# A decoder layer's opening: row products taken before the norm, the norm put in at their eviction, loads in another order, TensorE given transposes at the start

## The chip, the cores and the metric

The kernel runs on one core of one Trainium2 chip. The metric is device time in microseconds (us), taken over the whole program; fewer is better. Five engines work side by side, each through its own list of instructions in a fixed order: TensorE (PE: matmuls and transposes), VectorE (DVE), ScalarE (ACT), GpSimd (POOL) and SyncE (SP, which here issues the loads). They wait for each other by semaphores. PE writes into PSUM, which this kernel uses as eight banks of 128 x 512 floats: three with the tag `mm`, four with `at`, one with `o`. Everything else lives in SBUF.

## The reference, cut to what matters

A hybrid decoder layer on 512 rows of width 1024. What the change touches is the opening: the normed input `h`, its projections, and the keys and values of the memory.

```python
h = rms_norm(x, g_mix)                       # x * rsqrt(mean(x*x)) * g_mix, row by row
proj = h @ w_in                              # (512 x 1024) @ (1024 x PROJ_WIDTH)
q, k, v, qi, ki, wi, conv_in, qc, gate_pre = split_cols(proj, PROJ_SIZES)
qi, ki = partial_rope(qi), partial_rope(ki)  # index heads; score = sum_h wi * relu(qi . ki), top-256 keys
bg, cg, u = split(conv_in, 3)
y_conv = (bg * causal_dwconv(cg * u, conv_w_short)) @ w_conv_out
mem_kv = rms_norm(mem, g_mem) @ w_mem_kv     # keys and values of the 256 memory tokens
```

After that come attention, gates, an output projection, and a gated MLP with a causal convolution; the change leaves them as they are.

## The kernel before, in words

Every product is done in three matmuls. Both factors are split into a high part (the value rounded to the format fp32r) and a low part (what is left over), and `mm3` (L150 to L152) adds high x high, high x low and low x high. A split costs two instructions: ACT writes the high part (`whi`, `hhi`), DVE subtracts it from the source to give the low part (`wlo`, `hlo`). A projection `project(c0)` is 24 matmuls of 512 columns: eight slices k of the 1024 rows, three matmuls each, into one `mm` bank. The next weight tile is loaded by SP into one of three `raw` buffers and split by ACT and DVE.

The opening runs in this order. `x_n` holds, per slice k, the transposed x (512 columns), the 424 weight columns that need rows on the partitions (`wn`: v, the index queries and keys, and wi), and g_mix. `m_kv` holds the transposed memory, its 512 weight columns and g_mem.

1. The products of the memory (L295 to L299): 48 matmuls into two banks, `pkv[0]` (the `o` bank) and `pkv[1]` (an `mm` bank), as four loads of m_kv land.
2. The row norms: ACT squares the four tiles of x rows (L265), POOL takes the power (L269), DVE and ACT build a diagonal `dg`, high and low (L312, L315), and two matmuls with ones (L318) spread the norms over all partitions as `rb`, in PSUM.
3. For each slice k: DVE forms h = x * g_mix * rb (L345), ACT its high part (L348), DVE its low part (L351); every second k also splits `wn` (L347, L350). PE then does twelve matmuls of 424 columns (L354 to L358) into the four `at` banks. They are the row products, 96 in all. In between, ACT squares the two tiles of memory rows and evicts `kr` and `VM` from the two `pkv` banks.
4. The projections of the short convolution, three passes c over C_CG, C_U and C_BG. For c = 0 the three weight tiles are loaded ahead (`ahead`, L320 to L330). C_CG is evicted by ACT as `rr` (L520), C_U multiplied with it by DVE (L523), C_BG multiplied in later. PE's ten transposes of `rn` (the index queries and keys after rope, L390 and L392) come two matmuls after the start of C_U.
5. ACT lays the index queries and keys out for four-way packed products (`Q4`, `K4`, L444 and L455, with DMAs from SP for the low parts), and PE does the score matmuls (L463) in between the next projections.

What sets the order: the instructions in `keep(...)` stay in the order in which they are written; the others are placed by a scheduler that goes by its own model of when things are ready. On each engine the result is a fixed list. `bank("mm")` gives out three buffers; a product into a bank waits until what was in it has been read.

Of the kernel before, what the change touches and what calls it, by code (L numbers as in the profile page):

```python
# [93 lines left out]
def layer(ctx, tc, x, mem, g_ffn, g_final, w_in, x_n, m_kv, w_cm, w_att, w_o, w_up, w_down,  # L94
# [150 lines left out]
    mkv, rows = [], []
    for c in range(KD // 2):
        n = 1 if c == 0 else 2
        raw = op.tile([P, 2, M + 2 * CW + 1], F32, tag=kv_tags[c], name="mkv")
# [3 lines left out]
        if c == 2:
            rows += [first_rows(x, b, wp, "raw", 3) for b in range(2)]
    rows += [first_rows(x, 2, wp, "raw", 3), first_rows(x, 3, op, "omeh")]
    xn = []
    for c in range(KD // 2):
        raw = ea.tile([P, 2, S + NW + 1], F32, name=f"xn{c}")
        keep(nc.sync.dma_start(raw, x_n[2 * c:2 * c + 2].rearrange("k p c -> p k c")))
        xn.append(raw)
# [56 lines left out]
    rb = bank()  # L316
    for i in range(2):
        keep(nc.tensor.matmul(rb, ones_r, dg[:, i].rearrange("p b s -> p (b s)"), start=i == 0, stop=i == 1))  # L318

    ready = {}  # L320

    def ahead(c0):

        src = w_in[IN_STARTS.index(c0)]
        raw = wp.tile(list(src.shape), F32, tag="raw", name="raw", bufs=3)
        keep(nc.sync.dma_start(raw, src))
        hi = wp.tile(list(src.shape), F32R, tag="whi", name="whi", bufs=3)
        lo = wp.tile(list(src.shape), F32R, tag="wlo", name="wlo", bufs=3)
        keep(nc.scalar.activation(hi, raw, AF.Copy))
        keep(nc.vector.tensor_sub(lo, raw, hi.bitcast(F32)))  # L330
        ready[c0] = hi, lo


    kr = op.tile([P, MB, CW], F32, tag="oath", name="kr")
    rm = ea.tile([P, MB], F32, name="rm")
    vms = [pkv[b][:, CW:].rearrange("p (h d) -> p h d", d=HD) for b in range(MB)]
    pn = [bank("at") for b in range(NB)]
    for c, raw in enumerate(xn):
        wh = ea.tile([P, 2, NW], F32R, name=f"wnh{c}")
        wl = ea.tile([P, 2, NW], F32R, name=f"wnl{c}")  # L340
        w = raw[:, :, S:S + NW]
        for j in range(2):
            k = 2 * c + j
            xt = raw[:, j, :S]
            keep(nc.vector.scalar_tensor_tensor(xt, xt, raw[:, j, S + NW:], rb, op0=ALU.mult, op1=ALU.mult))  # L345
            if j == 0:
                keep(nc.scalar.activation(wh, w, AF.Copy))  # L347
            keep(nc.scalar.activation(h[0][:, k], xt, AF.Copy))  # L348
            if j == 0:
                keep(nc.vector.tensor_sub(wl, w, wh.bitcast(F32)))  # L350
            keep(nc.vector.tensor_sub(h[1][:, k], xt, h[0][:, k].bitcast(F32)))  # L351
            bs = [slice(b * P, (b + 1) * P) for b in range(NB)]
            for b in range(NB):
                keep(nc.tensor.matmul(pn[b][:, :NW], h[0][:, k, bs[b]], wh[:, j], start=k == 0, stop=False))  # L354
            for b in range(NB):
                keep(nc.tensor.matmul(pn[b][:, :NW], h[0][:, k, bs[b]], wl[:, j], start=False, stop=False))  # L356
            for b in range(NB):
                keep(nc.tensor.matmul(pn[b][:, :NW], h[1][:, k, bs[b]], wh[:, j], start=False, stop=k == KD - 1))  # L358

            if k in (4, 5):  # L360
                squares(memn[k - 4], ss[:, 1, k - 4:k - 3])
            if k == 5:
                power(ss[:, 1, :MB], rm)
            if k == 6:
                for b in range(MB):
                    keep(nc.scalar.activation(kr[:, b], pkv[b][:, :CW], AF.Copy, scale=rm[:, b:b + 1]))
                    keep(nc.scalar.activation(VM[:, b, :, 0:HD], vms[b], AF.Copy, scale=rm[:, b:b + 1]))
# [1 line left out]
    for b in range(MB):
        keep(nc.vector.scalar_tensor_tensor(VM[:, b, :, HD:], vms[b], rm[:, b:b + 1], VM[:, b, :, 0:HD].bitcast(F32),  # L370
                                            op0=ALU.mult, op1=ALU.subtract))
    rn = op.tile([P, NB, NIH + 1, IDXD], F32, tag="ocvl", name="rn")
# [540 lines left out]
```

## Time and profile before

| | us |
|---|---|
| time, median of 3 runs (lowest, highest) | 758.69 (757.86, 758.94) |
| the profiled execution's own time | 758.13 |
| its span in the trace | 756.3 |
| PE busy | 739.1 (98%) |
| DVE busy | 466.8 (62%) |
| ACT busy | 341.2 (45%) |

The profiled execution is one of its own; its 758.13 lies between the lowest and the highest of the three runs, 0.56 us below their median. The span goes from the first to the last instruction of the trace. In the slices of the page PE is at 9 tenths or more from the third of 40 slices to the last but one; only the first 38 us and the last slice have room. All that the change moves lies in the first 75 us.

### The profile page before, as it was taken

How to read it: one execution, taken by the hardware profiler on the slowest of the kernel's cores; microseconds unless marked ns; L12 is line 12 of the kernel's file. 1: busy time of each engine (PE TensorE's matmuls, PEld its weight loads, DVE VectorE, ACT ScalarE, POOL GpSimd, SP SyncE). 2: the span in 40 equal slices, each digit the busy share in tenths (PEclk: the TensorE clock that was granted, in tenths of full speed). 3: DMA queues.
4: the chain of work that ended last, by engine and by line, in shares of the span. 5: the costliest groups of instructions: out<-in, count | busy, mean ns of one | idle time of the engine just before them, and what ended most of it. 6: DMA issues, size and time to landing. Idle time of an engine off the chain costs nothing.

```text
span 756.3 us, 9061 instructions
## 1 busy us (share of the span) xinstructions
PE 739.1 (98%) x3428; PEld 616.7 (82%) x3428; DVE 466.8 (62%) x787; ACT 341.2 (45%) x566; POOL 17.4 (2%) x42
## 2 busy tenths in 40 slices
PE   6899999999999999999999999999999999999995
PEld 4788888888888888888899888888888888888884
DVE  4756999999777763385466565656565654121215
ACT  6658465686455543244235434343434343121214
POOL 0100002000000000000010000000000000000001
PEclk9999999999999999999999999999999999999998
DMA  9725234522122224244403232322223232323202
GB/s 340 285 95 181 84 113 125 168 66 81 56 92 74 73 74 177 92 140 140 139 29 102 94 100 96 94 101 90 105 87 109 86 110 81 114 84 111 84 28 112
DMA packets 25931, 83.37 MB, mean 110 GB/s; under 512 B 3264, under 2 KB 4416, under 8 KB 25888
## 3 DMA queue, kind: packets, MB, share of 16 engines
q1 hardware_dynamic: 25744, 82.53, 32.6%
q8 instruction: 27, 0.44, 0.2%
q10 hardware_dynamic: 144, 0.26, 0.1%
q14 instruction: 16, 0.13, 0.1%
HBM read 77.34 MB, written 2.10 MB: 105 GB/s over the span
## 4 chain that ended last, share of the span: by engine, by line
PE 95%; DMA 1%; ACT 1%; DVE 1%; issue 0%; POOL 0%; SPq 0%; POOLq 0%; ACTq 0%
PE ps_mm L151 19%; PE ps_mm L150 19%; PE ps_mm L152 19%; PE ps_at L150 9%; PE ps_at L152 9%; PE ps_at L151 9%; DMA mkv<-m_kv 1%; PE ps_at L668 1%; PE ps_o L699 1%; PE ps_at L354 1%; PE ps_at L356 1%; PE ps_at L358 1%; PE ps_at L685 1%; PE ps_o L152 1%; PE ps_o L151 1%; PE ps_o L150 1%
## 5 line engine op out<-in xcount | busy, mean ns | idle before, releaser
L161 DVE TENSOR_TENSOR wlo<-raw,whi 128x1024 fp32r<-128x1024 f32 (+2 forms) x122 | 144.7, 1187 | 193.0 <-ACT whi L160 192.9
L160 ACT ACTIVATE whi<-raw 128x1024 fp32r<-128x1024 f32 (+2 forms) x122 | 125.8, 1032 | 181.2 <-PE ps_o L152 82.3
L150 PE MATMUL ps_mm<-hhi,whi 128*128 128x512 f32 x312 | 122.4, 392 | 0.0
L151 PE MATMUL ps_mm<-hlo,whi 128*128 128x512 f32 x312 | 122.1, 391 | 0.0
L152 PE MATMUL ps_mm<-hhi,wlo 128*128 128x512 f32 x312 | 122.1, 392 | 0.0
L151 PE MATMUL ps_at<-h2l,whi 128*128 128x512 f32 (+1 forms) x216 | 78.9, 366 | 0.0
L152 PE MATMUL ps_at<-h2h,wlo 128*128 128x512 f32 (+1 forms) x216 | 78.8, 365 | 0.0
L150 PE MATMUL ps_at<-h2h,whi 128*128 128x512 f32 (+1 forms) x216 | 78.7, 366 | 0.0
L151 PEld LDWEIGHTS ps_mm<-hlo,whi 128*128 128x128 f32 x312 | 58.6, 188 | 11.6
L152 PEld LDWEIGHTS ps_mm<-hhi,wlo 128*128 128x128 f32 x312 | 58.6, 188 | 11.6
L150 PEld LDWEIGHTS ps_mm<-hhi,whi 128*128 128x128 f32 x312 | 58.6, 188 | 11.5
L150 PE MATMUL ps_mm<-h2h,whi 128*128 128x512 f32 x160 | 62.2, 389 | 0.0
L151 PE MATMUL ps_mm<-h2l,whi 128*128 128x512 f32 x160 | 62.2, 389 | 0.0
L152 PE MATMUL ps_mm<-h2h,wlo 128*128 128x512 f32 x160 | 62.2, 389 | 0.0
L151 PEld LDWEIGHTS ps_at<-h2l,whi 128*128 128x128 f32 x216 | 40.7, 189 | 6.6
L152 PEld LDWEIGHTS ps_at<-h2h,wlo 128*128 128x128 f32 x216 | 40.7, 189 | 6.5
L150 PEld LDWEIGHTS ps_at<-h2h,whi 128*128 128x128 f32 x216 | 40.6, 189 | 6.5
L151 PEld LDWEIGHTS ps_mm<-h2l,whi 128*128 128x128 f32 x160 | 30.0, 188 | 6.3
L152 PEld LDWEIGHTS ps_mm<-h2h,wlo 128*128 128x128 f32 x160 | 30.0, 188 | 6.2
L150 PEld LDWEIGHTS ps_mm<-h2h,whi 128*128 128x128 f32 x160 | 30.0, 188 | 6.2
L832 ACT ACTIVATE t<-t 128x512 f32<-128x512 f32 x22 | 13.9, 633 | 44.8 <-DVE t L514 44.7
L160 ACT ACTIVATE acth<-t 128x512 fp32r<-128x512 f32 x14 | 8.8, 632 | 40.4 <-DVE t L833 40.4
(276 smaller groups left out, 1296.0 us busy)
## 6 DMA issues: line engine op xcount, KB each, us to landing
raw<-w_up SPq DMA_DIRECT2D x44, 512.0 KB, 3.5
raw<-w_in SPq DMA_DIRECT2D x39, 512.0 KB, 3.3
raw<-w_down SPq DMA_DIRECT2D x22, 512.0 KB, 3.4
raw<-w_o SPq DMA_DIRECT2D x8, 512.0 KB, 3.5
xn<-x_n SPq DMA_DIRECT2D x4, 937.0 KB, 13.9
raw<-w_cm SPq DMA_DIRECT2D x8, 320.0 KB, 2.9
mkv<-m_kv SPq DMA_DIRECT2D x3, 769.0 KB, 8.4
rows<-x SPq DMA_DIRECT2D x4, 512.0 KB, 10.8
```

The lines of the kernel that those rows point to most:

```text
L150: nc.tensor.matmul(o, sh, mh, start=first, stop=False)
L151: nc.tensor.matmul(o, sh, ml, start=False, stop=False)
L152: nc.tensor.matmul(o, sl, mh, start=False, stop=last)
L160: nc.scalar.activation(hi, src, AF.Copy)
L161: nc.vector.tensor_sub(lo, src, hi.bitcast(F32))
L354: keep(nc.tensor.matmul(pn[b][:, :NW], h[0][:, k, bs[b]], wh[:, j], start=k == 0, stop=False))
L356: keep(nc.tensor.matmul(pn[b][:, :NW], h[0][:, k, bs[b]], wl[:, j], start=False, stop=False))
L358: keep(nc.tensor.matmul(pn[b][:, :NW], h[1][:, k, bs[b]], wh[:, j], start=False, stop=k == KD - 1))
L668: nc.tensor.matmul(pb[:, :N], QS[:, hd, b * P:(b + 1) * P], KS[i][:, g, :N], start=(i == 0), stop=(i == 1))
L685: nc.tensor.transpose(pt[:, kb * P:(kb + 1) * P], lt[:, kb * P:(kb + 1) * P], ident)
L699: nc.tensor.matmul(po[:, q0:], V[:, kb, g, :], PT[i][:, c], start=(kb == 0 and i == 0), stop=(kb == NB - 1 and i == 1))
L832: nc.scalar.activation(tt[0], tt[0], AF.Silu)
```

## The change

The instructions of the row products no longer need the norms. Their factor is now x * g_mix, split into `xh` (ACT, with g_mix as its scale) and `xl` (DVE, one scalar_tensor_tensor). Since a row's norm is a factor of the whole row of the product, it is multiplied in where the product leaves PSUM: `rn`, `V` and `wiN` are each evicted times `rx`. `h` itself is still needed by every projection but one: it is built by `h_split(k)`, three instructions per k as before, in program order after and between the new splits. The exception is C_CG for c = 0: it too is computed from `xh` and `xl`, and DVE multiplies the result with `rb` (`cg0`); `rb` is copied from PSUM to SBUF by ACT for that.

Besides: PE begins with 15 transposes of the identity; the second m_kv load comes in two halves too; x_n comes ahead of most of the rows of x, and its second load in two halves; the loads of C_CG, of the rope table and of C_U come ahead of those of the memory rows; the norms of the memory rows and the eviction of `kr` and `VM`, and with it the release of both `pkv` banks, come after the set-up of Q4 and K4.

```diff
+    idle = bank("at")
+    for i in range(15):
+        keep(nc.tensor.transpose(idle[:, :P], ident, ident))
...
-        n = 1 if c == 0 else 2
+        n = 1 if c < 2 else 2
...
+    first_cols(0, 0, 2)
+    rows += [first_rows(x, b, wp, "raw", 3) for b in range(3)]
+    first_cols(1, 0, 1)
+    rows.append(first_rows(x, 3, op, "omeh"))
+    first_cols(1, 1, 1)
+    first_cols(2, 0, 2)
+    first_cols(3, 0, 2)
...
+    early(C_CG)
+    keep(nc.sync.dma_start(ropeN, rope_n))
+    early(C_U)
     memn = [first_rows(mem, 0, op, "omel"), first_rows(mem, 1, op, "omeh")]
-    keep(nc.sync.dma_start(ropeN, rope_n))
     keep(nc.sync.dma_start(par, params))
+    early(C_BG)
...
+    def cols_split(c, js):
...
+        keep(nc.scalar.activation(wh[:, sl], w, AF.Copy))
+        for j in js:
+            keep(nc.scalar.activation(xh[2 * c + j], raw[:, j, :S], AF.Copy, scale=raw[:, j, S + NW:]))
+        keep(nc.vector.tensor_sub(wl[:, sl], w, wh[:, sl].bitcast(F32)))
+        for j in js:
+            keep(nc.vector.scalar_tensor_tensor(xl[2 * c + j], raw[:, j, :S], raw[:, j, S + NW:], xh[2 * c + j].bitcast(F32),
+                                                op0=ALU.mult, op1=ALU.subtract))
...
+    def h_split(*ks):
+
+        for k in ks:
+            xt = xn[k // 2][:, k % 2, :S]
+            keep(nc.vector.scalar_tensor_tensor(xt, xt, xn[k // 2][:, k % 2, S + NW:], rb, op0=ALU.mult, op1=ALU.mult))
+            keep(nc.scalar.activation(h[0][:, k], xt, AF.Copy))
+            keep(nc.vector.tensor_sub(h[1][:, k], xt, h[0][:, k].bitcast(F32)))
...
+    rows_product(3, 2)
+    rb, cg0 = (lambda t: (t[:, 0], t[:, 1]))(g0p.tile([P, 2, S], F32, tag="g0", name="rb"))
+    cols_split(2, [0, 1])
+    keep(nc.scalar.activation(rb, pr, AF.Copy))
+    rows_products(4, 5)
+    h_split(0)
+    cols_split(3, [0, 1])
+    rows_products(6, 7)
+    h_split(1)
     ahead(C_CG)
...
+    h_split(2, 3, 4)
+
+    pc = bank()
+    for k in range(KD):
+        wh, wl = (x[:, k, :] for x in ready[C_CG])
+        for i, (a, b) in enumerate(((wh, xh[k]), (wh, xl[k]), (wl, xh[k]))):
+            keep(nc.tensor.matmul(pc, a, b, start=k == 0 and i == 0, stop=k == KD - 1 and i == 2))
...
     ahead(C_U)
+    h_split(5)
+    keep(nc.vector.tensor_mul(cg0, pc, rb))
+    h_split(6, 7)
+    ahead(C_BG)
...
+    rm = const.tile([P, MB], F32, name="rm")
+    for b in range(MB):
+        squares(memn[b], ss[:, 1, b:b + 1])
+    power(ss[:, 1, :MB], rm)
+    kr = op.tile([P, MB, CW], F32, tag="omel", name="kr")
...
+        keep(nc.scalar.activation(kr[:, b], pkv[b][:, :CW], AF.Copy, scale=rm[:, b:b + 1]))
...
     for c in range(3):
         taps = [cvS[:, 3 * j + c:3 * j + c + 1] for j in range(3)]
-        pc = project(C_CG + c * P)
-        cg = rp.tile([P, S], F32, tag="rr", name="rr", bufs=2)
-        nc.scalar.activation(cg, pc, AF.Copy)
+        if c == 0:
+            cg = cg0
+        else:
+            pc = project(C_CG + c * P)
+            cg = rp.tile([P, S], F32, tag="rr", name="rr", bufs=2)
+            nc.scalar.activation(cg, pc, AF.Copy)
```

How the lists of the engines stand at the places that matter. Names: `xn` is the loaded x_n (x in place, h after L345 or L360), `xg` the new xh and xl, `raw` a weight tile as loaded, `rn` the index rows. First DVE, before, at the end of the row products up to the first weight tiles:

```order
L351 TENSOR_TENSOR hlo<-xn_138,hhi 128x512 [waits Activation_49]
L345 SCALAR_TENSOR_TENSOR xn_140<-xn_140,ps_mm 128x512 [waits DMAHW4_49]
L350 TENSOR_TENSOR wnl_367<-xn_140,wnh_366 128x848 [waits Activation_49]
L351 TENSOR_TENSOR hlo<-xn_140,hhi 128x512 [waits Activation_49]
L345 SCALAR_TENSOR_TENSOR xn_140<-xn_140,ps_mm 128x512
L351 TENSOR_TENSOR hlo<-xn_140,hhi 128x512 [waits Activation_49]
L330 TENSOR_TENSOR wlo<-raw,whi 128x1024 [waits DMAHW1_49,Activation_49]
```

And DVE in the changed kernel, from the last split of x to the eviction of rn:

```order
L340 TENSOR_TENSOR wnl<-xn_146,wnh 128x848 [waits DMAHW6_49,Activation_49]
L342 SCALAR_TENSOR_TENSOR xg_269<-xn_146,xg_268 128x512 [waits Activation_49] x2
L360 SCALAR_TENSOR_TENSOR xn_143<-xn_143,rb 128x512
L362 TENSOR_TENSOR hlo<-xn_143,hhi 128x512 [waits Activation_49]
L369 TENSOR_TENSOR wlo<-raw,whi 128x1024 [waits DMAHW7_49,Activation_49]
L360 SCALAR_TENSOR_TENSOR xn_144<-xn_144,rb 128x512
L362 TENSOR_TENSOR hlo<-xn_144,hhi 128x512 [waits Activation_49]
L360 SCALAR_TENSOR_TENSOR xn_144<-xn_144,rb 128x512
L362 TENSOR_TENSOR hlo<-xn_144,hhi 128x512 [waits Activation_49]
L360 SCALAR_TENSOR_TENSOR xn_145<-xn_145,rb 128x512
L362 TENSOR_TENSOR hlo<-xn_145,hhi 128x512 [waits Activation_49]
L419 TENSOR_SCALAR rn<-ps_at,rx 128x288 [waits PE_49] x2
```

Five of the eight h slices now stand ahead of the eviction of rn, each with a subtraction that waits for ACT; the other three (k = 5 to 7) stand behind the rope and the low part of C_U. Before, all eight stood ahead of the first weight tile. Next PE, before, at the start of C_U:

```order
L150 MATMUL ps_mm<-hhi,whi 128x512 [waits Activation_49]
L151 MATMUL ps_mm<-hlo,whi 128x512
L392 MATMUL ps_at<-ident,rn 128x128 [waits DVE_49,PE_49,Pool_49]
L392 MATMUL ps_at<-ident,rn 128x128 x5
L390 MATMUL ps_at<-ident,rn 32x128 [waits PE_49]
L390 MATMUL ps_at<-ident,rn 32x128 x3
L152 MATMUL ps_mm<-hhi,wlo 128x512 [waits DVE_49]
```

And PE in the changed kernel behind CG of the second pass, some 80 instructions further on (`K_539` and `Q_538` are the packed index keys and queries):

```order
L152 MATMUL ps_mm<-hhi,wlo 128x512
L525 MATMUL ps_at<-K_539,Q_538 128x256 [waits DMAHW5_49,DMAHW4_49,DMAHW6_49,DMAHW3_49,Activation_49]
L525 MATMUL ps_at<-K_539,Q_538 128x256 [waits DMAHW7_49,DMAHW0_49,PE_49]
L525 MATMUL ps_at<-K_539,Q_538 128x256 [waits DMAHW2_49,DMAHW1_49,PE_49]
L525 MATMUL ps_at<-K_539,Q_538 128x256 [waits DMAHW7_49,DMAHW6_49,PE_49]
L525 MATMUL ps_at<-K_539,Q_538 128x256 [waits DMAHW1_49,DMAHW0_49,DVE_49]
L150 MATMUL ps_mm<-hhi,whi 128x512 [waits Activation_49]
L151 MATMUL ps_mm<-hlo,whi 128x512
```

The order around the transposes is the same in both. What is new is that five score matmuls stand ahead of C_U of the second pass, and that its first matmul waits for ACT; before, PE's list had that projection as follows (its first eight matmuls and the four scores that stand inside it):

```order
L150 MATMUL ps_mm<-hhi,whi 128x512 [waits DVE_49,Activation_49]
L151 MATMUL ps_mm<-hlo,whi 128x512
L152 MATMUL ps_mm<-hhi,wlo 128x512 [waits DVE_49]
L150 MATMUL ps_mm<-hhi,whi 128x512
L151 MATMUL ps_mm<-hlo,whi 128x512
L152 MATMUL ps_mm<-hhi,wlo 128x512
L150 MATMUL ps_mm<-hhi,whi 128x512
L151 MATMUL ps_mm<-hlo,whi 128x512
L463 MATMUL ps_at<-K_479,Q_478 128x256 [waits DMAHW5_49,DMAHW4_49,DMAHW6_49,DMAHW1_49,DMAHW0_49]
L463 MATMUL ps_at<-K_479,Q_478 128x256 [waits DMAHW3_49,DMAHW2_49,PE_49]
L463 MATMUL ps_at<-K_479,Q_478 128x256 [waits PE_49]
L463 MATMUL ps_at<-K_479,Q_478 128x256 [waits DMAHW7_49,PE_49]
```

Its first matmul then waited for DVE's product with C_U of the first pass (L523), which frees the bank, and for its own weights; now it waits for ACT to evict CG of the second pass (`rr`, L585), since that is the bank it writes.

Last ACT in the changed kernel, the end of its queue ahead of the eviction of CG of the second pass (`rr`, L585); `hvh` is the high part of rQ, `rows` a square of memory rows, `rs` the convolution's first tap:

```order
L160 ACTIVATE hvh<-rQ 128x384
L504 ACTIVATE Q_538<-rQ 32x384 x11
L493 ACTIVATE K_539<-rK 32x512
L504 ACTIVATE Q_538<-rQ 32x384 x4
L160 ACTIVATE hvh<-rQ 128x384
L504 ACTIVATE Q_538<-rQ 32x384
L287 ACTIVATE rows,ss<-rows 128x1024
L160 ACTIVATE whi<-raw 128x1024
L287 ACTIVATE rows,ss<-rows 128x1024
L590 ACTIVATE rs<-rb,par 128x512
L160 ACTIVATE whi<-raw 128x1024
L585 ACTIVATE rr<-ps_mm 128x512
```

Before, the same queue of copies stood ahead of that eviction, without the two squares, which were done among the row products. Of the three `mm` banks one (`pkv[1]`) is not released until `kr` and `VM` are evicted, four instructions behind `rr`.

## Rows read from the trace of the kernel before

**Rows 1.** The page, part 1: busy us (share) and instructions of each engine.
```profile
PE 739.1 (98%) x3428; PEld 616.7 (82%) x3428; DVE 466.8 (62%) x787; ACT 341.2 (45%) x566; POOL 17.4 (2%) x42
```

**Rows 2.** Waits of PE: who waited for whom, total us, times, longest.
```profile
PE ps_o L295 <- ACT mT L285: 6.0, 3, 4.8
PE ps_at L354 <- ACT hhi L348: 1.5, 1, 1.5
```

**Rows 3.** Stretches: us, busy of PE, PEld, DVE, ACT, POOL, granted clock, DMA, GB/s.
```profile
10.00:15.00 5.00, 4.87 (x20) 3.68 (x21) 3.60 (x6) 4.27 (x8) 0.00 (x0) 1.00 1.03 415
...
25.00:26.00 1.00, 1.00 (x5) 0.93 (x4) 0.78 (x2) 0.18 (x1) 0.00 (x0) 0.50 1.04 418
```

**Rows 4.** Timeline of PE to 60 us: start, us, line, out<-in, idle before and releaser.
```profile
4.78 0.79 PE L295 MATMUL ps_o<-whi,mT 128*128 128x512 f32 x1 [4.78 <-ACT mT L285]
...
9.99 0.50 PE L295 MATMUL ps_o<-whi,mT 128*128 128x512 f32 x1 [0.88 <-ACT mT L285]
...
15.84 0.39 PE L299 MATMUL ps_mm<-whi,mT 128*128 128x512 f32 x1
...
24.29 1.45 PE L354 MATMUL ps_at<-wnh,hhi 128*128 128x424 f32 x4 [1.50 <-ACT hhi L348]
...
28.25 0.94 PE L354 MATMUL ps_at<-wnh,hhi 128*128 128x424 f32 x4
...
44.49 0.40 PE L150 MATMUL ps_mm<-hhi,whi 128*128 128x512 f32 x1
...
49.98 0.39 PE L150 MATMUL ps_mm<-hhi,whi 128*128 128x512 f32 x1
```

**Rows 5.** The page, part 6: DMA issues, KB each, median us to landing.
```profile
xn<-x_n SPq DMA_DIRECT2D x4, 937.0 KB, 13.9
...
mkv<-m_kv SPq DMA_DIRECT2D x3, 769.0 KB, 8.4
rows<-x SPq DMA_DIRECT2D x4, 512.0 KB, 10.8
```

**Rows 6.** Timeline of ACT to 60 us.
```profile
8.48 1.06 ACT L282 ACTIVATE whi<-mkv 128x1024 fp32r<-128x1024 f32 x1 [2.40 <-DMA mkv<-m_kv]
...
10.55 1.06 ACT L282 ACTIVATE whi<-mkv 128x1024 fp32r<-128x1024 f32 x1 [0.21 <-DMA mkv<-m_kv]
...
12.31 1.05 ACT L265 ACTIVATE rows<-rows 128x1024 f32<-128x1024 f32 x1
...
20.95 1.28 ACT L315 ACTIVATE dg<-ident,rl 128x128 fp32r<-128x128 f32 x4 [1.91 <-DVE rl L310]
22.13 0.90 ACT L347 ACTIVATE wnh<-xn 128x848 fp32r<-128x848 f32 x1
23.60 0.63 ACT L348 ACTIVATE hhi<-xn 128x512 fp32r<-128x512 f32 x1 [0.57 <-DVE xn L345]
```

**Rows 7.** Timeline of DVE to 60 us.
```profile
36.92 1.04 DVE L350 TENSOR_TENSOR wnl<-xn,wnh 128x848 fp32r<-128x848 f32 x1 [0.50 <-ACT wnh L347]
...
38.48 0.74 DVE L345 SCALAR_TENSOR_TENSOR xn<-xn,ps_mm 128x512 f32<-128x512 f32 x1
39.93 0.69 DVE L351 TENSOR_TENSOR hlo<-xn,hhi 128x512 fp32r<-128x512 f32 x1 [0.70 <-ACT hhi L348]
40.88 1.23 DVE L330 TENSOR_TENSOR wlo<-raw,whi 128x1024 fp32r<-128x1024 f32 x1 [0.26 <-ACT whi L329]
...
44.11 0.84 DVE L376 COPY rn<-ps_at 128x288 f32<-128x288 f32 x2 [1.22 <-PE ps_at L358]
...
47.55 1.22 DVE L330 TENSOR_TENSOR wlo<-raw,whi 128x1024 fp32r<-128x1024 f32 x1
```

**Rows 8.** Timeline of PE, 60 to 85 us: the first matmul of C_U, second pass.
```profile
67.44 0.39 PE L150 MATMUL ps_mm<-hhi,whi 128*128 128x512 f32 x1
```

**Rows 9.** Timeline of ACT, 50 to 75 us.
```profile
50.96 0.87 ACT L396 ACTIVATE rQ<-ps_at 128x384 f32<-128x384 f32 x2
...
68.43 0.58 ACT L520 ACTIVATE rr<-ps_mm 128x512 f32<-128x512 f32 x1
```

More of the change, by code (lines that the diff above doesn't have):

```diff
@@ L251, in layer, with first_cols, early @@
         mkv.append(raw)
[L252 to L259, printed above, removed]
+    xn = [ea.tile([P, 2, S + NW + 1], F32, name=f"xn{c}") for c in range(KD // 2)]
+    def first_cols(c, i, n):
+        keep(nc.sync.dma_start(xn[c][:, i:i + n], x_n[2 * c + i:2 * c + i + n].rearrange("k p c -> p k c")))
+    first_cols(0, 0, 2)
[5 more added lines that the diff above has]
+    first_cols(3, 0, 2)
+    ready = {}
+    def early(c0):
+        src = w_in[IN_STARTS.index(c0)]
+        raw = wp.tile(list(src.shape), F32, tag="raw", name="raw", bufs=3)
+        keep(nc.sync.dma_start(raw, src))
+        ready[c0] = raw
+    early(C_CG)
+    keep(nc.sync.dma_start(ropeN, rope_n))
+    early(C_U)
     memn = [first_rows(mem, 0, op, "omel"), first_rows(mem, 1, op, "omeh")]
-    keep(nc.sync.dma_start(ropeN, rope_n))
     keep(nc.sync.dma_start(par, params))
+    early(C_BG)
     def squares(src, dst):
@@ L273, in layer @@
     mh, ml = mT[:, 0], mT[:, 1]
-    ss = ea.tile([P, 2, NB], F32, name="ss")
+    ss = const.tile([P, 2, NB], F32, name="ss")
     pkv = [bank("o"), bank()]
@@ L299, in layer @@
                     keep(nc.tensor.matmul(pkv[b], ml[:, k, bs[b]], hi[:, j], start=False, stop=k == KD - 1))
-        if c >= 2:
-            for b in (2 * c - 4, 2 * c - 3):
-                squares(rows[b], ss[:, 0, b:b + 1])
+    pn = [bank("at") for b in range(NB)]
+    xg = [op.tile([P, 3, S], F32R, tag=t, name="xg") for t in kv_tags] + [ea.tile([P, 2, S], F32R, name=f"xg{i}") for i in range(2)]
+    xh = [xg[k // 3 * 2][:, k % 3] for k in range(KD)]
+    xl = [xg[k // 3 * 2 + 1][:, k % 3] for k in range(KD)]
@@ new lines, in layer @@
+    wn = []
+    def cols_split(c, js):
+        raw = xn[c]
+        if js[0] == 0:
+            wn.append([ea.tile([P, 2, NW], F32R, tag="wn" + i, name="wn" + i, bufs=2) for i in "hl"])
+        wh, wl = wn[c]
+        sl = slice(js[0], js[-1] + 1)
+        w = raw[:, sl, S:S + NW]
+        keep(nc.scalar.activation(wh[:, sl], w, AF.Copy))
[5 more added lines that the diff above has]
+                                                op0=ALU.mult, op1=ALU.subtract))
@@ new lines, in rows_product, with rows_products @@
+    def rows_product(k, part):
+        w = wn[k // 2][part == 1][:, k % 2]
+        for b in range(NB):
+            keep(nc.tensor.matmul(pn[b][:, :NW], (xl if part == 2 else xh)[k][:, b * P:(b + 1) * P], w,
+                                  start=k == 0 and part == 0, stop=k == KD - 1 and part == 2))
+    def rows_products(*ks):
+        for k in ks:
+            for part in range(3):
+                rows_product(k, part)
+    def h_split(*ks):
+        for k in ks:
+            xt = xn[k // 2][:, k % 2, :S]
+            keep(nc.vector.scalar_tensor_tensor(xt, xt, xn[k // 2][:, k % 2, S + NW:], rb, op0=ALU.mult, op1=ALU.mult))
+            keep(nc.scalar.activation(h[0][:, k], xt, AF.Copy))
+            keep(nc.vector.tensor_sub(h[1][:, k], xt, h[0][:, k].bitcast(F32)))
@@ new lines, in ahead @@
+    def ahead(c0):
+        raw = ready[c0]
+        hi = wp.tile(list(raw.shape), F32R, tag="whi", name="whi", bufs=3)
+        lo = wp.tile(list(raw.shape), F32R, tag="wlo", name="wlo", bufs=3)
+        keep(nc.scalar.activation(hi, raw, AF.Copy))
+        keep(nc.vector.tensor_sub(lo, raw, hi.bitcast(F32)))
+        ready[c0] = hi, lo
+    cols_split(0, [0, 1])
+    rows_products(0, 1)
+    for b in range(3):
+        squares(rows[b], ss[:, 0, b:b + 1])
+    cols_split(1, [0])
+    rows_products(2)
@@ L305, in layer @@
+    squares(rows[3], ss[:, 0, 3:4])
     rx = ea.tile([P, NB], F32, name="rx")
@@ L308, in layer @@
     power(ss[:, 0], rx)
+    cols_split(1, [1])
     keep(nc.vector.tensor_copy(rh, rx))
     keep(nc.vector.tensor_sub(rl, rx, rh.bitcast(F32)))
-    dg = op.tile([P, 2, NB, P], F32R, tag="ocvh", name="dg")
+    dg = ea.tile([P, 2, NB, P], F32R, name="dg")
     keep(nc.vector.tensor_mul(dg[:, 0], ident.unsqueeze(1).to_broadcast([P, NB, P]),
@@ L315, in layer @@
         keep(nc.scalar.activation(dg[:, 1, b], ident, AF.Copy, scale=rl[:, b:b + 1]))
-    rb = bank()
+    rows_product(3, 0)
+    rows_product(3, 1)
+    pr = bank()
     for i in range(2):
[L318 to L331, printed above, removed]
@@ L334, in layer @@
[L334 to L367, printed above, removed]
@@ L368, in layer @@
-    ahead(C_CG)
[L369 to L372, printed above, removed]
+        keep(nc.tensor.matmul(pr, ones_r, dg[:, i].rearrange("p b s -> p (b s)"), start=i == 0, stop=i == 1))
+    rows_product(3, 2)
+    rb, cg0 = (lambda t: (t[:, 0], t[:, 1]))(g0p.tile([P, 2, S], F32, tag="g0", name="rb"))
@@ L396, in layer @@
             keep(nc.scalar.activation(rQ[:, t, :], pt[:, :SQ], AF.Copy))
-    ahead(C_BG)
     for b in range(NB):
-        split(V[:, b, :, 0:HD], V[:, b, :, HD:], pn[b][:, :KV].rearrange("p (g d) -> p g d", g=NG))
-        nc.vector.tensor_scalar_mul(wiN[:, b, :], pn[b][:, NW - NIH:NW], (NIH * IDXD) ** -0.5)
+        v = pn[b][:, :KV].rearrange("p (g d) -> p g d", g=NG)
+        nc.scalar.activation(V[:, b, :, 0:HD], v, AF.Copy, scale=rx[:, b:b + 1])
+        nc.vector.scalar_tensor_tensor(V[:, b, :, HD:], v, rx[:, b:b + 1], V[:, b, :, 0:HD].bitcast(F32), op0=ALU.mult,
+                                       op1=ALU.subtract)
+        nc.vector.tensor_scalar(wiN[:, b, :], pn[b][:, NW - NIH:NW], rx[:, b:b + 1], (NIH * IDXD) ** -0.5, op0=ALU.mult,
+                                op1=ALU.mult)
     def twice(K, r, j, hd, lo):
@@ L406, in twice @@
             move(K[1][c, hd, :], lo[a])
-    nc.vector.tensor_scalar_mul(bgT, bgT, 0.5)
+    keep(nc.vector.tensor_scalar_mul(bgT, bgT, 0.5))
     es.close()
@@ L456, in layer @@
                 move(Q4[64 + 32 * i:96 + 32 * i, 4 * t + j, :], ql[src])
+    rm = const.tile([P, MB], F32, name="rm")
[3 more added lines that the diff above has]
+    kr = op.tile([P, MB, CW], F32, tag="omel", name="kr")
+    for b in range(MB):
+        v = pkv[b][:, CW:].rearrange("p (h d) -> p h d", d=HD)
+        keep(nc.scalar.activation(kr[:, b], pkv[b][:, :CW], AF.Copy, scale=rm[:, b:b + 1]))
+        keep(nc.scalar.activation(VM[:, b, :, 0:HD], v, AF.Copy, scale=rm[:, b:b + 1]))
+        keep(nc.vector.scalar_tensor_tensor(VM[:, b, :, HD:], v, rm[:, b:b + 1], VM[:, b, :, 0:HD].bitcast(F32), op0=ALU.mult,
+                                            op1=ALU.subtract))
     for b in range(1, NB):
```

6 lines of the change are left out of this document (4 added, 2 removed).

## The prediction

> **What bounds the kernel now.** The page's first part gives PE 739.1 of 756.3 us [rows 1], so the kernel is bound by PE, and only what PE waits for can be won. The waits of PE name it: 6.0 us for the first memory operands (4.8 of them before the first matmul) and 1.5 us between norms and row products [rows 2]; no wait in it lies behind the start of the row products at 24.29 [rows 4]. So I read the timelines of PE, ACT and DVE over the first 75 us for two questions: how much earlier can PE run through the opening, and do the other engines keep up with it. An engine in whose shadow nothing waits today can become the wait tomorrow; only PE's position at a late, fixed point tells the net. I take the first matmul of C_U in the second pass, at 67.44 [rows 8], since PE's list is the same behind it but for the placing of score matmuls.
>
> **The opening, won.** The third pair of m_kv is on the chip when ACT begins its high part at 10.55 [rows 6]; the pair before was begun at 8.48 [rows 6] and its first matmul came at 9.99 [rows 4], 1.5 later. So now 10.55 + 1.5 = 12.1 for the third pair's first matmul. The fourth pair follows directly instead of behind two tiles of rows; at 0.415 MB/us [rows 3] its 0.787 MB (769 KB, [rows 5]) land 1.9 later, at 12.4, before PE needs it. Two pairs are 24 matmuls, which took 9.99 to 15.84 + 0.23 = 6.0 [rows 4]; the memory products end at 18.1. PE then goes straight into the row products, without the norms. At full clock 84 of the 96 went from 28.25 to 44.49 [rows 4], 0.773 for four; 24 such groups are 18.6, the two matmuls that spread the norms 0.5: C_CG starts at 37.1 instead of 44.49, 7.4 earlier. The 15 transposes and the half loads I put at nothing: PE sat idle to 4.78 anyway [rows 4], and the landing of the third pair ends the stretch with or without them. The cover lasts as long as the transposes end by 4.78; beyond, each would cost its own time.
>
> Do the operands come in time? After the third pair's landing at 10.5 follow 0.787 MB of m_kv, 0.959 MB of x_n, three tiles of rows of 0.524 MB, half of an x_n pair (0.480), the fourth tile of rows and the other half [rows 5]: 4.80 MB at 0.415 [rows 3] are 11.6, so k = 3 of x lands at 22.1. PE needs k = 2 at 18.1 + 6 x 0.773 = 22.7 and k = 3 at 25.0, after splits of some 2 us. Both hold, the second by less than a microsecond.
>
> The Trainium skill ("DMA: Bandwidth & Descriptors", Specifications) gives a core some 358 GB/s of HBM. By it the 4.80 MB would take 13.4 and k = 3 come at 23.9, which shifts the chain below by up to 1.8 us, for a sum of 767.1. The trace has 415 GB/s for five microseconds on end in this very stretch [rows 3], so I keep the measured rate; the page's figure lies within my range.
>
> **The lead, lost.** DVE gets nine more operations of 128 x 512 (eight xl and cg0) in the same list, the h slices come behind the splits of x, and each of them waits for ACT in its middle. The chain begins when the norms' diagonal is built. k = 3 at 22.1, its splits to 24.4 on DVE, the low part of the norms to 24.5; ACT then has 1.28 of diagonal and 0.90 of the next `wn` [rows 6]: 26.7, and DVE's `wnl` for k = 4, 5 begins at 26.8. From there, by durations: `wnl` 0.96 (36.92 to 37.88 by its row's 1.04 with a small overlap, [rows 7]); an xl 0.70, from the 0.74 of L345 [rows 7], whose operands it shares but for one; an h slice 38.48 to 39.93, and 0.69 of subtraction [rows 7], 2.1, of which 0.70 is the wait for ACT; `wlo` 1.23 with 0.26 of wait [rows 7], 1.5; rn, rope, V and wiN 44.11 to 47.55 [rows 7], 3.5.
>
> 0.96 + 1.4 + 2.1 (k = 4, 5 and h0) + 0.96 + 1.4 + 2.1 (k = 6, 7 and h1) + 1.5 (C_CG) + 6.3 (h2 to h4) + 3.5 (rn to rope) = 20.2, so the rope ends at 47.0. Then C_U's low part 1.2, h5 2.1, cg0 0.7, h6 and h7 4.2: 55.2, with ACT's last high part at 54.5; C_BG's low part 1.5: 56.7.
>
> PE against it: C_CG takes 44.49 to 49.98, 5.5 [rows 4], so 37.1 to 42.6. C_U's weights stand on ACT behind h4 and the eviction of rn: ready at 44.7, 2.1 of wait. Two matmuls on, the transposes want the rope: 47.0, 1.8 to 2.1 more. The last three slices of h, at 2.1 each against 0.7 of matmuls, and C_BG's low part at 56.7 take the rest: 22 matmuls at 0.229 later C_BG is done at 61.7, CG of the second pass 5.5 later, at 67.2. Today C_U follows at 67.44: the 7.4 are used up, almost to the tenth, by waits that did not exist.
>
> **And more.** At this point PE now waits for something new: C_U's first matmul for ACT's eviction of CG (`rr`), behind five score matmuls. On ACT the copies from `rQ` to `rr` took 50.96 to 68.43 [rows 9], 17.5 almost without idle time, and the same ones stand there now (five high parts of weights, sixteen of Q, the rest alike), plus two squares of memory rows at 1.05 [rows 6]. They begin when ACT is through with h7, 54.5, not 50.96: 54.5 + 17.2 + 2.1 = 73.8, `rr` ends at 74.4. PE stands there from 67.2, less the scores (five of 256 columns, half of 0.229 each, 0.6). C_U begins at 74.4, 7.0 late, and 0.6 of scores are behind it rather than ahead: **+6.4**. That the five scores need Q4 and K4, which I estimate at 70 to 72 from the same queue, lies inside this wait.
>
> What is not in a row: xh with a scale from memory against the plain copy of 0.63 [rows 6]; bounds 0.63 and 0.9 (the copy of `wn`), taken 0.7; eight of them cost ACT at most 2 us before 35, beside its idle time. The copy of `rb`, one eviction, 0.6, hidden likewise. An h slice with rb in SBUF: between 0.69 and 0.74 for its first product, taken as the latter; 0.4 less over eight.
>
> **The clock.** From 19.9 to 24.29 PE did two matmuls; then the granted clock was 0.50 of 2.4 GHz, its lower level, from 25 on [rows 3], and the first twelve products took 24.29 to 28.25, 3.96 instead of 3 x 0.773 = 2.32 [rows 4]: 1.6 lost. That fall goes, and is in the 7.4. A wait of some 6 us before 74.4 may bring one back: 0 to 1.6, I take 0.8. A fall in the waits near 45 costs nothing, since DVE sets the pace there.
>
> **Sum.** 758.13 (the profiled execution; span 756.3; 0.56 under the median of the runs shown, the same within their spread) + 6.4 + 0.8 = **765.3**. Own range 761.5 to 768: clock (-0.8 to +0.8), h slices (-0.4), and some 2 us either way for the start of the chain.
>
> **Rivals.**
> *The hand-offs don't add up.* DVE's list runs without the eight waits of 0.70 for ACT, because ACT is ahead. Then the chain ends 5.6 earlier, ACT gets to `rQ` at 48.9 and `rr` ends at 68.8: +0.8 and no fall, 758.9, no change. For it: ACT is idle for over half of the row products today. Against: the subtraction follows its own slice in the list, so nothing fills the gap; in the rows, too, the wait comes in every second slice, the others being filled by `wnl`. It decides from where h7 is done by 48.5, and with slices that also start earlier it goes below 758. Chance 0.12.
> *The lead holds.* DVE and ACT stay ahead of PE altogether, and the eviction of `rr` with them: 758.13 - 7.4 = 750.7. For it: PE has 7.5 us of waits to give. Against: 27.7 us of DVE chain between 26.8 and 54.5, where PE has 18 of work. With shares of it (752 to 757): chance 0.11.
> *Worse.* The clock falls in full, the loads land 2 us later than the rate of [rows 3] says, or kr, VM and the scores behind `rr` keep `mm` banks and ACT busy into the second C_BG: 768 to 772, chance 0.15.
> *Forecast*: 0.62.
>
> **Numbers.** 0.2% is 1.5 us; less can't be told from no change here. Faster (under 756.6): 0.11 and a little of the first rival, 0.13. Same: the rest of the first rival, and a forecast whose second wait is nearly gone, 0.13. Slower 0.74. Range 757 to 769.5: below it 0.11, above it 0.08.
>
> **What would show it.** In the profile after: first row product near 18, C_CG (L413) near 37; PE idle at 42 to 47 for ACT `whi` and DVE `rn` (L427), short waits for L361, L362 and L369 to 57; CG of the second pass done near 67; then PE waiting to 74 for the DMAs of Q4 and K4 and for ACT `rr` (L585), and nothing later. If C_U of the second pass begins before 68, the term of ACT's queue is wrong; if PE does not wait at the transposes, DVE's chain is.

## The result, and the profile after

The changed kernel takes 766.31 us (median of 4 runs, 766.03 to 766.72) against 758.43 for the one before: ratio 1.0104, 95% interval 1.0087 to 1.0122. It is slower by 7.9 us; 765.3 was forecast. The profiled execution's span is 764.2 us. The page's first part for PE, to be held against [rows 1]:

```profile
PE 745.3 (98%) x3443; PEld 620.8 (81%) x3443; DVE 473.2 (62%) x798; ACT 346.9 (45%) x576; POOL 18.0 (2%) x42
```

PE is 6.2 us longer busy with 15 more instructions. The 15 new transposes alone are 3.5 of that, at the start, where PE had nothing to do before; the rest is not split up here, since PE works at a lower clock in some stretches of both kernels. The waits of PE (who waited for whom, total us, times, longest):

```profile
PE ps_at L439 <- DVE rn L427: 2.4, 1, 2.4
PE ps_mm L150 <- ACT rr L585: 2.2, 1, 2.2
PE ps_mm L150 <- ACT whi L368: 1.6, 1, 1.6
PE ps_at L246 <- POOL ident masks.py:199: 1.5, 1, 1.5
PE ps_at L525 <- DMA K<-kl: 1.4, 1, 1.4
PE ps_at L525 <- DMA Q<-hvl: 1.4, 2, 0.9
PE ps_mm L152 <- DVE wlo L369: 0.3, 1, 0.3
PE ps_mm L151 <- DVE hlo L362: 0.2, 1, 0.2
```

Both rows of [rows 2] are gone: no wait for the memory operands, none between norms and row products. In their place stand two new groups, one around the rope (`rn`, `whi`), one at the second pass (`K`, `Q`, `rr`). The timeline of PE gives their places; the rows answer to [rows 4] and [rows 8]:

```profile
17.40 0.94 PE L348 MATMUL ps_at<-wnh,xg 128*128 128x424 f32 x4
...
36.39 0.62 PE L413 MATMUL ps_mm<-xg,whi 128*128 128x512 f32 x2
...
43.72 0.50 PE L150 MATMUL ps_mm<-hhi,whi 128*128 128x512 f32 x1 [1.63 <-ACT whi L368]
...
46.86 1.43 PE L439 MATMUL ps_at<-ident,rn 128*128 128x128 f32 x6 [2.41 <-DVE rn L427]
...
66.49 0.39 PE L152 MATMUL ps_mm<-hhi,wlo 128*128 128x512 f32 x1
...
68.31 0.61 PE L525 MATMUL ps_at<-K,Q 128*128 128x256 f32 x3 [1.43 <-DMA K<-kl]
69.39 0.36 PE L525 MATMUL ps_at<-K,Q 128*128 128x256 f32 x1 [0.48 <-DMA Q<-hvl]
70.69 0.40 PE L525 MATMUL ps_at<-K,Q 128*128 128x256 f32 x1 [0.94 <-DMA Q<-hvl]
73.28 0.79 PE L150 MATMUL ps_mm<-hhi,whi 128*128 128x512 f32 x1 [2.19 <-ACT rr L585]
...
77.71 0.39 PE L151 MATMUL ps_mm<-hlo,whi 128*128 128x512 f32 x1
```

Read it as a ledger of PE's lead. C_CG starts at 36.39 instead of 44.49: 8.1 won. CG of the second pass ends at 66.7, when C_U of that pass would have begun at 67.44 before: 0.7 of the 8.1 is left. C_U begins at 73.28: 5.8 behind. The ten matmuls from 73.28 to 77.71 take 4.4 where ten at 0.229 take 2.3: 2.1 for the clock. 5.8 + 2.1 less the five scores already done (0.6) is 7.3 of the 7.9. At the first product of the convolution's result (`ocvh`, 197.78 before, 205.24 after) the loss stands at 7.5; the last 0.4 comes later and is not followed here. The columns of the stretches are as in [rows 3]:

```profile
10.00:15.00 5.00, 4.78 (x20) 3.27 (x19) 4.03 (x6) 4.44 (x8) 0.00 (x0) 1.00 1.03 414
...
45.00:50.00 5.00, 3.14 (x13) 2.73 (x14) 4.31 (x14) 0.63 (x1) 0.00 (x0) 0.70 0.22 66
...
70.00:75.00 5.00, 2.12 (x5) 1.62 (x6) 4.36 (x5) 5.00 (x13) 0.90 (x2) 0.59 0.39 98
75.00:80.00 5.00, 5.00 (x18) 3.97 (x18) 3.16 (x8) 1.30 (x4) 0.00 (x0) 0.73 0.52 176
```

PE is busy for 2.12 of the five microseconds from 70, ACT for all of them: it is the engine that is waited for. Granted clock 0.59 and 0.73 mark the stretch at the lower level behind the wait. On DVE the chain of the prediction stands as forecast, 0.7 us earlier at its start and 0.3 at the end of the rope:

```profile
26.07 1.04 DVE L340 TENSOR_TENSOR wnl<-xn,wnh 128x848 fp32r<-128x848 f32 x1 [1.61 <-ACT wnh L337]
...
34.34 0.69 DVE L362 TENSOR_TENSOR hlo<-xn,hhi 128x512 fp32r<-128x512 f32 x1 [0.70 <-ACT hhi L361]
...
46.42 0.30 DVE L427 TENSOR_TENSOR rn<-rn,rt 128x144 f32<-128x144 f32 x1
```

The seven other h slices have the same 0.70 (once 0.69) ahead of their subtraction. And on ACT, from the last high part of h to the eviction that PE waits for:

```profile
53.25 0.63 ACT L361 ACTIVATE hhi<-xn 128x512 fp32r<-128x512 f32 x1 [1.43 <-DVE xn L360]
...
68.05 1.06 ACT L287 ACTIVATE rows<-rows 128x1024 f32<-128x1024 f32 x1
...
72.66 0.57 ACT L585 ACTIVATE rr<-ps_mm 128x512 f32<-128x512 f32 x1
```

From 53.25 on ACT has no idle time in this view; what stands between is the queue that took 50.96 to 68.43 before [rows 9], and the squares.

### The profile page after: what moved, and what is told of

Read it like the earlier page. It is cut to its first block, busy times and chain, and to the rows that moved or that the text cites. A ratio compares the mean times of both kernels' runs of the same rounds, so it can differ in the third digit from the quotient of the medians.

```text
span 764.2 us, 9125 instructions
## 1 busy us (share of the span) xinstructions
PE 745.3 (98%) x3443; PEld 620.8 (81%) x3443; DVE 473.2 (62%) x798; ACT 346.9 (45%) x576; POOL 18.0 (2%) x42
## 4 chain that ended last, share of the span: by engine, by line
PE 88%; ACT 3%; DVE 2%; issue 1%; POOL 0%; POOLq 0%; ACTq 0%
PE ps_mm L150 18%; PE ps_mm L151 18%; PE ps_mm L152 18%; PE ps_at L150 9%; PE ps_at L152 9%; PE ps_at L151 9%; ACT Q L504 1%; PE ps_at L733 1%; PE ps_o L764 1%; PE ps_at L750 1%; PE ps_o L152 1%; PE ps_o L151 1%; PE ps_o L150 1%; PE ps_at L664 0%; PE ps_o L702 0%
## 5 line engine op out<-in xcount | busy, mean ns | idle before, releaser
L150 PE MATMUL ps_mm<-hhi,whi 128*128 128x512 f32 x304 | 120.8, 397 | 3.8 <-ACT rr L585 2.2
L152 PE MATMUL ps_mm<-hhi,wlo 128*128 128x512 f32 x304 | 120.3, 396 | 0.3 <-DVE wlo L369 0.3
L151 PE MATMUL ps_mm<-hlo,whi 128*128 128x512 f32 x304 | 120.3, 396 | 0.2 <-DVE hlo L362 0.2
```

What stands on the lines that cost most here:

```text
L150: nc.tensor.matmul(o, sh, mh, start=first, stop=False)
L151: nc.tensor.matmul(o, sh, ml, start=False, stop=False)
L152: nc.tensor.matmul(o, sl, mh, start=False, stop=last)
```

## The experiments

Each is compared with the kernel before in the same session (758.3); where a gain against the changed kernel is given, that is its median of 766.31. The first five take one suspect away, or put one into the kernel before. The theory under test, called two-stall theory below: the waits at the rope eat the lead, and the held bank with ACT's queue makes a second stall behind it.

**Memory norms early.**

```diff
-    h_split(2, 3, 4)
+    h_split(2)
+    squares(memn[0], ss[:, 1, 0:1])
+    h_split(3)
+    squares(memn[1], ss[:, 1, 1:2])
+    h_split(4)
+    power(ss[:, 1, :MB], rm)
...
     ahead(C_U)
+    for b in range(MB):
+        keep(nc.scalar.activation(kr[:, b], pkv[b][:, :CW], AF.Copy, scale=rm[:, b:b + 1]))
...
```

> The changed kernel with the squares of the memory rows between the h slices (k = 2 to 4) and kr and VM evicted behind the split of C_U's weights, so that the third mm bank is free before the second pass. Two-stall theory: C_U of the second pass no longer waits for ACT's eviction of CG, the 5.8 us by which it starts late and the two us of low clock behind it go, the wait for the rope stays: 766.3 - 7.3 = 759. Rival 1 (ACT's queue alone, the bank doesn't matter): only the two squares of 1.05 come off the queue, 764.2. Rival 2 (all of the loss is made at the rope and the h slices, the rest is an echo): 766.3.

Measured 757.31 (756.83 to 757.83), ratio to before 0.9986 (0.9978 to 0.9995). That is 9.0 less than the changed kernel, 1.7 more than expected, and no wait of PE in the list begins behind 56 us. The waits of PE (without a last one of 0.2 us at the start):

```profile
PE ps_at L453 <- DVE rn L433: 1.6, 1, 1.6
PE ps_mm L150 <- ACT whi L368: 1.6, 1, 1.6
PE ps_at L246 <- POOL ident masks.py:199: 1.5, 1, 1.5
PE ps_mm L152 <- DVE wlo L369: 0.5, 2, 0.3
```

The first square, at 38.38, stands in what was idle time of ACT, and so does the second, at 40.44; the eviction of CG still comes late, and PE shows no wait for it, since C_U writes another bank:

```profile
38.38 1.04 ACT L287 ACTIVATE rows<-rows 128x1024 f32<-128x1024 f32 x1
...
70.30 0.57 ACT L587 ACTIVATE rr<-ps_mm 128x512 f32<-128x512 f32 x1
```

So the first rival (queue alone, 764.2) falls. Squares and bank were moved together here; the next run takes them apart.

**Only the squares early**, kr and VM still behind Q4 and K4.

> The changed kernel with the squares of the memory rows early, as in e1_mem_early, but kr and VM still evicted behind the set-up of Q4 and K4 (they now stand ahead of CG's eviction on ACT, and C_U of the second pass takes their bank). Two-stall theory: what counts is when a bank is free. Of ACT's queue the two squares (2.1) are gone and four evictions (1.4) come in: C_U starts near 71.5 instead of 73.28, 1.8 less, with the clock still falling: 764 to 764.8. Rival (the squares alone were the cost): all of the second stall goes but what the scores' DMAs hold, 70.69: 2.6 less and the clock with it, 761.5 to 763.7.

Measured 763.97 (ratio 1.0075, 1.0063 to 1.0087). By the time alone this is just at the edge of the two-stall theory (764 to 764.8) and 0.3 above the rival; the timeline of PE decides: C_U waits for the bank of kr and VM and starts at 71.52, 1.8 earlier than in the changed kernel, as forecast.

```profile
70.88 0.36 PE L527 MATMUL ps_at<-K,Q 128*128 128x256 f32 x1 [0.91 <-DMA Q<-hvl]
71.52 0.80 PE L150 MATMUL ps_mm<-hhi,whi 128*128 128x512 f32 x1 [0.29 <-DVE vm L519]
```

Of the 9.0 us that the early norms give, the squares alone are 2.3; the other 6.7 come with the early release of the bank.

**DVE evicts CG** in the second and third pass.

```diff
-            nc.scalar.activation(cg, pc, AF.Copy)
+            nc.vector.tensor_copy(cg, pc)
```

> The changed kernel with CG of the second and third pass copied out of PSUM by DVE instead of ACT; the bank of the memory products is still held. Two-stall theory: the copy leaves ACT's queue; C_U of the second pass then starts behind three scores, whose DMAs let them go at 68.3 and 69.4, so near 69.7 instead of 73.28: 3.6 less, and 0 to 2 of clock, 761 to 763. Rival (the DMAs of Q4 and K4 are what holds PE, not the eviction): the last of the five scores went at 70.69, so at most 2.6 less without any clock, 763.7 to 764.5. Rival 2 (echo of the rope): 766.3.

Measured 760.75 (ratio 1.0032, 1.0019 to 1.0044), 0.25 below what the two-stall theory gave. With the bank still held, taking the copies of CG out of ACT's queue is worth 5.6. C_U starts behind three scores, at full clock:

```profile
68.80 0.61 PE L525 MATMUL ps_at<-K,Q 128*128 128x256 f32 x3 [1.58 <-DMA K<-kl]
69.24 0.40 PE L150 MATMUL ps_mm<-hhi,whi 128*128 128x512 f32 x1
```

**h slices interleaved**: the first product of a slice goes ahead of the subtraction of the slice before.

```diff
-    h_split(2, 3, 4)
+    h_up(3)
+    h_low(2)
+    h_up(4)
+    h_low(3)
+    h_up(5)
+    h_low(4)
```

> The changed kernel with DVE's first product of an h slice issued ahead of the subtraction of the slice before it, so that DVE does not stand 0.70 us in each slice for ACT. Two-stall theory: seven waits of 0.70 leave DVE's chain, the rope and h7 are done up to 4.9 us earlier, ACT reaches its queue as much earlier, and C_U of the second pass starts near 68.5 to 69.5: 761 to 762.5. Rival (hand-offs cost nothing, the queue is set by ACT's own work): 766.3. Rival 2 (the queue starts with the transposes, which wait for the rope alone): 2 to 3 us less, 763.5.

Measured 761.14 (ratio 1.0040, 1.0028 to 1.0053), 5.2 less than the changed kernel and within the range of the two-stall theory; the profiled execution, at 762.23, is the slowest of the five and 3.8 below the profiled one of the changed kernel. The start of C_U moves by 3.3, to 70.01, where 68.5 to 69.5 had been expected. The wait for ACT remains, with a granted clock of 0.66 from 70 to 75 us:

```profile
67.27 0.71 PE L537 MATMUL ps_at<-K,Q 128*128 128x256 f32 x4 [2.12 <-DMA K<-kl]
...
70.01 0.50 PE L150 MATMUL ps_mm<-hhi,whi 128*128 128x512 f32 x1 [1.42 <-ACT rr L597]
```

Of the 4.9 us of hand-offs 3.3 arrive here: ACT's queue of copies begins 3.3 earlier (52.38 against 55.69) and waits there for PE's transposes, which stand later in PE's list in this kernel. So the limit that the second rival names is there, though its time (763.5) did not come:

```profile
52.38 0.87 ACT L455 ACTIVATE rQ<-ps_at 128x384 f32<-128x384 f32 x2 [1.09 <-PE ps_at L451]
```

**The kernel before with late memory norms.**

```diff
-            if k in (4, 5):
-                squares(memn[k - 4], ss[:, 1, k - 4:k - 3])
...
+    for b in range(MB):
+        squares(memn[b], ss[:, 1, b:b + 1])
+    power(ss[:, 1, :MB], rm)
```

> The kernel before with only one part of the change: memory squares and the eviction of kr and VM behind the set-up of Q4 and K4, the bank held until then. Two-stall theory: PE's lead is nought there, so C_U of the second pass waits for what ACT's queue delays, 2.1 of squares and 1.4 of evictions: 3.3 to 3.8 us late, plus 0 to 1.6 of clock, 758.4 + 3.3 to 5.4 = 762 to 764. Rival 1 (ACT has room and catches up): 758.4, no change. Rival 2 (only the bank matters, not the squares): C_U waits for the product with C_BG alone, 1 us or less: 759.

Measured 765.34 as median of six, 761.42 in the profiled execution; ratio 1.0097 (1.0082 to 1.0111). One part of the change, put into the kernel before, makes a stall at the same place, through another instruction: the squares hold up the first convolution tap on ACT, DVE's list stands behind that, and the fifth score wants a bank from DVE:

```profile
68.59 0.43 PE L461 MATMUL ps_at<-K,Q 128*128 128x256 f32 x1 [3.44 <-DVE sc L463]
69.28 0.76 PE L150 MATMUL ps_mm<-hhi,whi 128*128 128x512 f32 x1 [0.26 <-ACT rr L518]
```

3.7 of waits, as expected; the median is 1.3 above the expected range, the profiled execution 0.6 below it. That execution need not stand for the others: its opening ran 2.9 us ahead of the profile before (C_CG at 41.60 instead of 44.49), with a granted clock of 1.00 from 25 to 30 us, where the kernel before has 0.50 at 25 [rows 3]. The five runs without a trace are 3 to 5 us above it and have mean granted clocks of 0.989 to 0.993 against 0.995. What loads and clock did in them can't be seen; that part is open.

**Without the transposes**, on top of the early memory norms.

> e1_mem_early (757.31) without the 15 transposes. DVE-chain theory: the memory products run longer at the lower clock and end about a microsecond later, C_CG starts as much later, but C_U's weights and the rope are not ready before 44.4 and 46.7 in any case: 757.3, no change. Rival (the clock at the start is worth its time): the two microseconds and more of half speed that the kernel before shows at 4.78 to 7.5 come back, 758.3 to 758.9.

Measured 757.46 (756.72 to 757.95) against 757.31: no difference. PE first works at 4.83 and waits 1.0 instead of 1.6 for C_U's weights.

**The second m_kv load in one piece**, likewise.

> e1_mem_early (757.31) with the second m_kv load in one piece. DVE-chain theory: the third pair's high part began at 9.81 in the changed kernel against 10.55 before; if the halves are what brought that, PE is 0.7 later up to C_CG, and the chain on DVE keeps its start, since x comes behind the same bytes: 757.3 to 757.6. Rival (the whole stream of loads is faster for it, the norms' chain too): 758.0 to 758.1.

Measured 758.84 (756.78 to 759.36): 1.5 more than with halves, more than either theory said. PE stands 2.4 us at 10.30 for the second pair, the granted clock of the five microseconds from 10 is 0.66, and C_CG begins at 39.70 instead of 37.03. The two matmuls that spread the norms stand in PE's list behind the row products, so `rb` comes later as well, and DVE's first h slice waits for it. The expectation had DVE's chain keep its start:

```profile
10.30 0.50 PE L317 MATMUL ps_o<-whi,mT 128*128 128x512 f32 x1 [2.42 <-ACT mT L307]
30.48 0.75 DVE L360 SCALAR_TENSOR_TENSOR xn<-xn,rb 128x512 f32<-128x512 f32 x1 [1.07 <-ACT rb L400]
```

C_U begins at 45.85 instead of 44.36. Of these 1.5, 1.1 are this wait and 0.3 a later landing of the loads (`wnl` at 27.04 instead of 26.70). The runs fall in two groups by mean granted clock, 756.8 to 758.2 at 0.994 to 0.998 and 758.8 to 759.4 at 0.992, and the profiled one, at 759.22, is of the second. What the opening looked like in the first group is not shown.

**Both stalls treated**: early memory norms and interleaved slices.

> e1_mem_early and e3_pipe together. Two-stall theory: the second stall is gone by e1, and of the lead of 7.4 that the first one eats, DVE's shorter chain gives back what of its seven waits of 0.70 lies ahead of PE's waits: 2.4 to 4.9 less than e1, 752.4 to 754.9. Rival (without the second stall PE has other waits for ACT's weights, which don't depend on the hand-offs): 756 to 757.

Measured 756.20 (755.15 to 756.31), ratio 0.9966 (0.9954 to 0.9979): the gain over the early norms is 1.1, not 2.4 to 4.9. The rival (756 to 757) was right: C_U still waits for its weights, which stand on ACT and DVE behind the slices.

```profile
PE ps_mm L152 <- DVE wlo L372: 1.3, 1, 1.3
PE ps_mm L150 <- ACT whi L371: 1.3, 1, 1.3
```

The granted clock from 45 to 50 us, around and behind the second of them, is 0.66.

**And the weights of C_CG and C_U split first.**

```diff
-    h_up(1, 2)
-    h_low(1)
     ahead(C_CG)
+    h_up(1)
+    h_up(2)
+    h_low(1)
+    ahead(C_U)
...
-    ahead(C_U)
```

The cut is against the kernel one step behind; C_U's split comes from behind the rope, and h6, left out here, moves ahead of the rope.

> c13_early_pipe with the splits of C_CG's and C_U's weights moved ahead of h1 and of h3, and h6 ahead of the rope. Two-stall theory: PE's waits for C_U's weights (1.6 for ACT in e1, 1.6 for DVE in e3) go, the transposes still wait for the rope, which comes later by the moved work: 1 to 2 less than c13_early_pipe, 751.5 to 753.5. Rival (DVE's chain sets the time whatever stands first in it): the same as c13_early_pipe.

Measured 754.01 (753.83 to 754.59), ratio 0.9942 (0.9929 to 0.9954): 4.3 faster than the kernel before, 12.3 faster than the changed one. It is 0.5 above the expected range, which was set before the time of the kernel one step behind was known; against that kernel the gain is 2.2, for 1 to 2 expected. Both waits for C_U's weights are gone, and behind 12 us the list shows 2.0 us of waits for PE:

```profile
PE ps_at L465 <- DVE rn L445: 1.5, 1, 1.5
PE ps_at L246 <- POOL ident masks.py:199: 1.5, 1, 1.5
PE ps_o L317 <- ACT mT L307: 0.8, 2, 0.6
PE ps_mm L151 <- DVE hlo L365: 0.5, 1, 0.5
```

DVE's slices now run with no gap, 1.27 us each instead of 2.05:

```profile
39.79 0.68 DVE L365 TENSOR_TENSOR hlo<-xn,hhi 128x512 fp32r<-128x512 f32 x1
40.39 0.74 DVE L359 SCALAR_TENSOR_TENSOR xn<-xn,rb 128x512 f32<-128x512 f32 x1
41.05 0.68 DVE L365 TENSOR_TENSOR hlo<-xn,hhi 128x512 fp32r<-128x512 f32 x1
```

**The same without the transposes.**

> c13c_weights_first (754.01) without the 15 transposes. There PE reaches C_U's weights without a wait and stands 1.5 for the rope and 0.5 for an h slice. DVE-chain theory: PE is a microsecond later up to C_U and waits that much less at the rope: 754.0, within 0.5. Rival (PE is the bound up to the rope, so the warm start is worth its microsecond): 755.0 to 755.5.

Measured 754.12 (753.70 to 755.56): no difference here either. The profiled execution took 755.26. PE's waits at the rope are those of the run with the transposes (1.4 and 0.5), but the granted clock from 50 to 55 us is 0.66 (first row) where that run has 1.00 (second row):

```profile
50.00:55.00 5.00, 4.63 (x13) 3.73 (x14) 4.95 (x9) 5.00 (x9) 0.00 (x0) 0.66 0.27 98
50.00:55.00 5.00, 4.88 (x19) 3.37 (x20) 4.95 (x9) 4.99 (x10) 0.00 (x0) 1.00 0.34 107
```

## Why the prediction was right, by its own steps

- *The sum.* 6.4 + 0.8 was forecast. C_U's delay less the scores came to 5.8 - 0.6 = 5.2, the clock to 2.1, and 0.6 of the 7.9 lie elsewhere. The path was right; that the total came within 1.0 is in part luck, since the two terms missed by 1.2 and 1.3 in opposite directions.
- *Opening, 7.4 won.* 8.1 were. The third pair's high part began at 9.81, where 10.55 was taken, and the row products and C_CG were 0.7 ahead of their forecasts too. That the half loads brought this is not shown: with halves that high part begins between 9.77 and 10.47 in nine profiles, with the load in one piece at 9.21, 10.55 and 10.76 in three. So the 0.7 lies within what executions differ by. The reason behind "half loads at nothing", that the third pair's landing ends the stretch with or without them, did fail: with the load in one piece PE waits 2.4 for the second pair and is 2.7 later at C_CG, the low clock behind that wait included. "Transposes at nothing" held in the two kernels that were run without them, to 0.2.
- *Loads.* The measured rate held: 414 GB/s from 10 to 15 us, and ACT begins on k = 3 at 21.63 (landing forecast for 22.1). The Trainium skill's 358 GB/s ("DMA: Bandwidth & Descriptors", Specifications) does not describe this stretch, and the term of 1.8 that hung on it did not come.
- *DVE's chain.* 26.8 to 47.0 was forecast for the start of `wnl` and the end of the rope, 26.07 to 46.7 measured; each slice has its wait of 0.70. In all ten profiles of the changed kernel and its variants `wnl` begins 16.25 to 16.29 after the third pair's high part (16.25 forecast), so the start of this chain moves with the loads. That the waits are the term, not DVE's work, is shown by the interleaved slices (5.2 less in the median, 3.8 in the profiled execution).
- *The lead used up.* CG of the second pass ends at 66.7 (67.2 forecast).
- *ACT's queue and the bank.* C_U at 73.28 (74.4 forecast; 0.6 to 0.7 of the difference comes from the earlier start). The runs with early norms, with squares alone and with DVE's eviction each move this start to where the list of waits says.
- *The clock*, taken as 0.8 with 1.6 as the upper bound, cost 2.1. This is the mis-sized term: the bound came from a fall after 4.4 us with two matmuls in it, this one came after 6.6 with five scores in it. The fall near 45 came too (0.70) and cost nothing, as said: PE still waits for DVE behind it, 0.2 at 54.66 and 0.3 at 56.14.
- *Rivals.* "The hand-offs don't add up" is refuted by the 0.70 in each slice and the run without them. "The lead holds" came halfway true only once the weights, the slices and the bank were dealt with: the fastest kernel is then 4.3 ahead of the one before, of the 8.1.

## What to carry to other kernels

A lead won for the bounding engine at the start is only worth what the other engines can hold: find a late, fixed instruction of that engine and ask which queue releases it. Work that is moved out of a busy place takes its buffers along: two squares and four evictions, put later, held a PSUM bank and cost more (9.0) than the whole opening gave (8.1). In a chain over two engines, issue the next slice's first half ahead of this slice's second, and put operands that the bounding engine wants first at the head of the list.
